# Weights split by accumulating DMAs from GpSimd's queue, and buffers that begin at multiples of 1 KB

## The chip, the cores and the metric

The kernel runs on one core of one Trainium2 chip. The metric is the device time of one execution in microseconds; the time before is the median of three runs. Traces are of one profiled execution on that core.

## What is computed

Two transformer-like blocks in a row on one sequence of 512 tokens of width 1024, all in float32: a block with gated linear attention, three groups of dilated attention, a mixing projection, an MLP and a gated embedding; and a block of two layers, one with mLSTM and stick-breaking attention, one with multi-scale pooling. Cut to the matmuls that carry the time:

```python
def first_block(x, p, ln1, w_in, ...):
    h = rmsnorm(x, ln1[i])
    hq, hk, hv, hr, ha, hatt, hgate = _split_cols(h @ w_in[i], SPLIT_SIZES)
    ...                                   # gla_mixer, dilated_attention x 3
    mix = (jax.nn.sigmoid(g_gla) * y_gla + jax.nn.sigmoid(g_att) * y_att) @ w_out[i]
    x = x + mix
    h2 = rmsnorm(x, ln2[i])
    x = x + jnp.square(jax.nn.relu(h2 @ w_mlp1[i])) @ w_mlp2[i]
    h3 = rmsnorm(x, ln3[i])
    x = x + jax.nn.sigmoid(h3 @ w_pg[i]) * (p[i] @ w_pp[i])
    return rmsnorm(x, ln_f)

def even_layer(...):   # mlstm, stick_breaking
    u = h @ w_in
    ...
    y = jnp.concatenate([ya, yb], axis=-1) @ w_out
    return x + rmsnorm_2(y, post_g)

def odd_layer(...):    # h @ w_in, multiscale_pool, grouped matmul, @ w_out
```

## The kernel before

**Precision.** Every large product is made of three matmuls in fp32r, a rounded form of float32: an operand is split into a high part (rounded to fp32r) and a low part (the rest), and high times high, high times low and low times high are summed in PSUM. `split` (L168) does this for activations: ACT copies with rounding, DVE subtracts. A matmul has 128x128 weights (the stationary operand) and 512 columns of the moving operand.

**Weights.** The host lays all weights out as a stream of chunks of 128x1024 float32 (512 KB), in the order of use; the kernel takes 316 of them. `load_chunk` (L206) loads a chunk by a DMA from SP's queue into a buffer of the ring `raw` (three buffers). `split_chunk` (L213) makes the parts in the rings `wh` and `wl` (four buffers each): ACT copies with rounding (L219), DVE subtracts (L220), and the next load is issued, which waits until that subtract has freed its raw buffer.

**Units.** One unit of work consumes one chunk: 24 matmuls with 512 columns. In `fm` (L330) the weights are stationary and the activations move; in `tok` (L411) the activations are stationary and the weights move. `run` (L284) goes through the program's groups of one to three units; ahead of a group that begins with unit i it calls `split_chunk(i + 3)` (L300), then lets side jobs (attention, gated linear attention, mLSTM, stick-breaking) take their next step by `pump` (L272), then emits the unit's matmuls, and after these the evacuation of its PSUM bank. Side jobs have fixed lags, counted in units (`LAG`). A scheduler then orders each engine's instructions.

**Buffers.** Activations lie in buffers of 2 KB a partition, in three kinds: e (44 buffers), s and r (16 each). In the built program the e buffers and the weight rings begin at 320 bytes past a multiple of 1 KB in each partition, the s and r buffers at 672 bytes past one: the first is a multiple of 64 bytes, the second lies 32 bytes past such a multiple. The products with the MLP's second weights (L780 and L782) read their moving operand from s and r buffers (L757), those with the first weights (L761) from e buffers; the last products (`w_out_c_2`, by `tok`) read their stationary operand from s and r buffers (L1470). Of the 7,534 matmuls with 512 columns in the built program, 1,576 have an operand that begins 32 bytes past a multiple of 64: 1,192 the moving one, 448 the stationary one (64 of them both). With the change there are 26.

**GpSimd (POOL)** has few instructions: the triangular masks of the side jobs (`causal`, L193, a select on 128x128 or 128x256), adds of squares for the norms (`accum`, L499), and a copy in `narrow` (L362). No DMA is issued from its queue. All work of the helper `mm` is at L162, of `act` at L124, of `tt` (the subtracts among it) at L141, of `stt` at L153.

**The start.** `setup` (L508) issues, on SP's queue, the vectors, x's first tile, the first 256 columns of chunks 0 and 1, x's second tile, the other 768 columns, the other six tiles of x, and then chunks from 2 on. `prologue` (L549) splits them in that order, pinned, and chunk 2 after these.

## Time and profile before

| | |
|---|---|
| time, median of 3 runs | 1937.28 us (1932.48 to 1937.69) |
| the profiled execution | 1936.63 us, span of its trace 1934.9 us |
| PE (matmuls) busy | 1911.9 us, 99% of the span |
| PEld (weight loads into the array) busy | 1597.9 us, 83% |
| DVE busy | 1090.2 us, 56% |
| ACT busy | 873.2 us, 45% |
| POOL busy | 94.7 us, 5% |
| DMA | 184.32 MB, mean 95 GB/s |
| granted clock of TensorE | 0.996 of full speed |

Busy time of PE includes the overlap of pipelined matmuls: one of 512 columns is shown with some 390 ns, but a new one begins every 225 to 235 ns in a stretch without idle time, so how many instructions fall into a stretch says more than the busy time. Idle time of an engine is given with what ended it. An engine that is busy 56% of the time may still be the one that PE waits for in a short stretch.

### The profile page before, as it was taken

Reading aid. Unit: us, or ns where it says so; the run is one execution under the profiler, and the core shown is the slowest. Engines: PE = TensorE matmul, PEld = TensorE weight load, DVE = VectorE, ACT = ScalarE, POOL = GpSimd, SP = SyncE. Lnnn points to the kernel's source line nnn. Section 1 sums busy time; section 2 is a strip of 40 time slices with the busy share of each in tenths; the row PEclk is TensorE's granted clock in tenths of the full one; section 3 lists DMA queues with packets and bytes.
Section 4 is the critical chain, followed back from the end, with each engine's and each line's share of the span. In section 5 each row is a group of like instructions: output and inputs, shape, how many; then the busy total and the mean of one; then the engine's idle time right before and its main releaser. Section 6 shows DMA issues by size and latency. Waiting matters only on the chain.

```text
span 1934.9 us, 22678 instructions
## 1 busy us (share of the span) xinstructions
PE 1911.9 (99%) x8894; PEld 1597.9 (83%) x8894; DVE 1090.2 (56%) x1623; ACT 873.2 (45%) x1274; POOL 94.7 (5%) x125
## 2 busy tenths in 40 slices
PE   8999999999999999999998999999999999999998
PEld 7888888888888888888887888888888888888886
DVE  5235544677446433444556768677866627666723
ACT  4233344564234321342355666767666534423321
POOL 0000000000001000000120000111100011000000
PEclk9999999999999999999999999999999999999999
DMA  5342222122242322333232323222222322233222
GB/s 182 126 106 87 83 77 98 66 77 88 92 138 87 109 98 92 107 98 98 88 115 81 120 77 91 73 88 77 88 87 74 126 96 76 87 98 98 96 92 74
DMA packets 68095, 184.32 MB, mean 95 GB/s; under 512 B 17058, under 2 KB 20815, under 8 KB 67988
## 3 DMA queue, kind: packets, MB, share of 16 engines
q1 hardware_dynamic: 67412, 181.82, 29.2%
q8 instruction: 70, 1.15, 0.2%
q10 hardware_dynamic: 576, 1.05, 0.1%
q14 instruction: 37, 0.30, 0.1%
HBM read 178.55 MB, written 6.12 MB: 95 GB/s over the span
## 4 chain that ended last, share of the span: by engine, by line
PE 94%; DVE 3%; ACT 1%; DMA 1%; issue 0%; SPq 0%; POOL 0%; DVEq 0%; ACTq 0%; POOLq 0%
PE t L162 93%; DVE t L141 2%; ACT t L124 1%; DMA t<-t 1%; DVE t L153 1%; PE t L965 0%; DMA t<-wstream 0%; PE t L1528 0%; ACT L124 0%; POOL t L499 0%; PE t L1037 0%; SPq L528 0%; ACT L135 0%; DVE t L1252 0%; SPq L525 0%
## 5 line engine op out<-in xcount | busy, mean ns | idle before, releaser
L162 PE MATMUL t<-t,t 128*128 128x512 f32 (+3 forms) x8532 | 1871.5, 381 | 15.7 <-ACT t L124 9.8
L162 PEld LDWEIGHTS t<-t,t 128*128 128x128 f32 x8532 | 1550.0, 192 | 323.2 <-ACT t L124 13.4
L141 DVE TENSOR_TENSOR t<-t,t 128x1024 fp32r<-128x1024 f32 (+9 forms) x982 | 773.1, 815 | 730.4 <-ACT t L124 404.1
L124 ACT ACTIVATE t<-t 128x1024 fp32r<-128x1024 f32 (+6 forms) x883 | 633.5, 758 | 924.3 <-PE t L162 557.6
L153 DVE SCALAR_TENSOR_TENSOR t<-t,ct,t 128x512 f32<-128x512 f32 (+5 forms) x128 | 102.5, 815 | 14.4 <-ACT t L124 11.2
L153 DVE SCALAR_TENSOR_TENSOR t<-t,t 128x512 f32<-128x512 f32 (+6 forms) x112 | 76.5, 702 | 54.2 <-PE t L162 45.8
L124 ACT ACT_TABLE_LOAD x69 | 88.5, 1283 | 11.2 <-DVE t L153 8.6
L499 POOL TENSOR_TENSOR t<-t,t 128x512 f32<-128x512 f32 x33 | 52.2, 1590 | 581.6 <-ACT t L124 581.3
L124 ACT ACTIVATE t<-t,t 128x128 f32<-128x128 f32 (+4 forms) x93 | 50.3, 545 | 62.8 <-PE t L162 36.7
L124 ACT ACTIVATE t<-t,ct 128x512 f32<-128x512 f32 (+5 forms) x89 | 54.8, 624 | 19.4 <-DVE t L141 12.8
L196 POOL TENSOR_SCALAR_AFFINE_SELECT t<-t 128x128 f32<-128x128 f32 x80 | 37.4, 482 | 418.3 <-ACT t L124 222.5
L141 DVE TENSOR_TENSOR t<-t 128x511 f32<-128x511 f32 (+5 forms) x64 | 37.3, 587 | 1.2
L473 DVE RECIPROCAL t<-t 128x512 f32<-128x512 f32 (+3 forms) x15 | 28.1, 1870 | 13.5 <-ACT t L124 13.5
L153 DVE SCALAR_TENSOR_TENSOR t<-t,t,t 128x512 fp32r<-128x512 f32 (+3 forms) x41 | 27.7, 683 | 13.1 <-ACT t L124 12.8
L162 PE MATMUL t<-t,ct 128*128 128x256 f32 (+4 forms) x142 | 28.6, 337 | 0.0
L162 PEld LDWEIGHTS t<-t,ct 128*128 128x128 f32 (+1 forms) x142 | 21.6, 186 | 3.6 <-issue 1.0
L130 ACT ACTIVATE t<-t 128x512 f32<-128x512 f32 (+2 forms) x25 | 12.4, 561 | 10.3 <-PE t L162 7.7
L162 PEld LDWEIGHTS t<-ct,t 128*128 128x128 f32 x112 | 16.5, 217 | 0.6
L132 ACT ACT_TABLE_LOAD x13 | 16.7, 1283 | 0.2
L162 PE MATMUL t<-ct,t 128*128 128x1 f32 (+1 forms) x112 | 16.2, 276 | 0.0
L1509 ACT ACTIVATE t<-t 128x512 f32<-128x512 f32 x8 | 4.8, 599 | 24.7 <-PE t L162 24.7
L135 ACT ACTIVATE t<-t 128x512 f32<-128x512 f32 (+2 forms) x29 | 15.8, 594 | 0.2
(54 smaller groups left out, 132.9 us busy)
## 6 DMA issues: line engine op xcount, KB each, us to landing
t<-wstream SPq DMA_DIRECT2D x314, 512.0 KB, 3.3
t<-xT SPq DMA_DIRECT2D x16, 256.0 KB, 5.3
xdram<-t SPq DMA_DIRECT2D x8, 256.0 KB
t<-udram SPq DMA_DIRECT2D x8, 256.0 KB
t<-xdram SPq DMA_DIRECT2D x8, 256.0 KB, 6.0
out<-t ACTq DMA_DIRECT2D x4, 256.0 KB, 2.1
out<-t SPq DMA_DIRECT2D x4, 256.0 KB
skew<-bdram SPq DMA_DIRECT2D x2, 510.0 KB
```

Source lines behind the costliest of these rows:

```text
L124: self.pinned(self.nc.scalar.activation(out, in_, func, **kw))
L130: last = self.nc.scalar.activation(o, x, AF.Abs, bias=bias)
L132: last = self.nc.scalar.preload_act_table_set(EXPLN)
L135: last = self.nc.scalar.activation(o, o, AF.Exp, scale=-1.0)
L141: self.pinned(self.nc.vector.tensor_tensor(out, a, b, op=op))
L153: self.pinned(self.nc.vector.scalar_tensor_tensor(out, a, s, b, op0=op0, op1=op1))
L162: self.nc.tensor.matmul(out, lhsT, rhs, start=start, stop=stop, skip_group_check=True)
L196: self.nc.gpsimd.affine_select(t[:, 0:n], t[:, 0:n], pattern=[[1, n]], compare_op=op, fill=0.0, base=base, channel_multiplier=-1)
L473: self.nc.vector.reciprocal(out, out)
L499: self.nc.gpsimd.tensor_tensor(st[key], st[key], sq, op=ALU.add)
L1509: last = nc.scalar.activation(sq, ps, AF.Square, accum_out=ss[j][:, c:c + 1])
```

## The change

- The ring `raw` and the loads on SP's queue are gone (but for chunks 0 and 1). A chunk's high part is loaded by a DMA on POOL's queue that writes fp32r, which rounds on the way.
- The low part: ACT writes the negated high part into the `wl` buffer (in place of the rounding copy), and a second DMA on POOL's queue reads the same chunk from HBM again and adds it to that buffer. DVE's subtract for 314 chunks is gone.
- The rings have five buffers in place of four. The high part of chunk i+4 is loaded, and the low part of chunk i+3 started, ahead of unit i.
- A pad and first uses of the buffer kinds place the buffers of 2 and 4 KB: in the built program all of e, s, r, `wh` and `wl` begin at multiples of 1 KB.
- At the start, chunks 0 and 1 come in three pieces (256, 256 and 512 columns) into s buffers.

```diff
--- before.py
+++ after.py
@@ -54,14 +54,14 @@
 ROUNDS = "a0 z0 a1 a2 z1 a3 z2 z3"
 BANKS = 2
 NCONST = P + 64 + P
-AHEAD = 4
+PAD = 88
 POOLSQ = 1
-PIECES = slice(0, 256), slice(256, 1024)
-HEAD = [("x", 0), ("w", 0), ("x", 1), ("w", 1)] + [("x", k) for k in range(2, KT)]
+PIECES = slice(0, 256), slice(256, 512), slice(512, 1024)
+HEAD = [("x", 0), ("w", 0), ("x", 1), ("w", 1), ("w", 2)] + [("x", k) for k in range(2, KT)]
 
 LAG = {'attention': (2, 5, 2), 'gla': (2, 3, 1, 2, 4), 'ml_gates': (5,), 'mlstm': (4, 0, 2), 'ml_out': (1, 0), 'stick': (0, 3, 3)}
 QBANKS, PER_SLOT = 4, 2
-RAW_BUFS, HL_BUFS = 3, 4
+HL_BUFS, LEAD = 5, 1
 BIASW = (383, 255, 255)
 N_ONEHOT = sum(BIASW)
 
@@ -203,24 +203,23 @@
         return h, l
 
 
+
+
     def load_chunk(self, j):
         while self.nd <= min(j, len(self.units) - 1):
-            t = self.sb.tile([P, 1024], F32, name=self._nm(), tag="raw", bufs=RAW_BUFS)
-            self.nc.sync.dma_start(t, self.io["wstream"][self.nd])
-            self.raw[self.nd] = t
+            h, l = (self.sb.tile([P, 1024], F32R, name=self._nm(), tag=t, bufs=HL_BUFS) for t in ("wh", "wl"))
+            self.nc.gpsimd.dma_start(h, self.io["wstream"][self.nd])
+            self.hl[self.nd] = h, l
             self.nd += 1
 
     def split_chunk(self, j):
         while self.ns <= min(j, len(self.units) - 1):
             self.load_chunk(self.ns)
-            raw = self.raw.pop(self.ns)
-            h = self.sb.tile([P, 1024], F32R, name=self._nm(), tag="wh", bufs=HL_BUFS)
-            l = self.sb.tile([P, 1024], F32R, name=self._nm(), tag="wl", bufs=HL_BUFS)
-            self.act(h, raw, AF.Copy)
-            self.sub(l, raw, h.bitcast(F32))
-            self.hl[self.ns] = (h, l)
+            h, l = self.hl[self.ns]
+            self.act(l, h.bitcast(F32), AF.Copy, scale=-1.0)
+            self.nc.gpsimd.dma_start(l, self.io["wstream"][self.ns], accum_op=ALU.add)
             self.ns += 1
-            self.load_chunk(self.ns - 1 + RAW_BUFS)
+            self.load_chunk(self.ns - 1 + LEAD)
 
 
     def load(self, dst, src):
@@ -297,7 +296,8 @@
                 x()
             else:
                 m = len(x)
-                self.split_chunk(i + HL_BUFS - 1)
+                self.split_chunk(i + HL_BUFS - 2)
+                self.load_chunk(i + HL_BUFS - 1)
                 for _ in range(m):
                     self.pump()
                     if self.jobs:
@@ -504,11 +504,22 @@
         self.act(z, z, AF.Silu)
         return z
 
+    def piece(self, j, k):
+        s = PIECES[k]
+        return self.raw[j][s.start // T][:, s.start % T:s.start % T + s.stop - s.start]
+
 
     def setup(self):
         nc, io = self.nc, self.io
         self.eps = self.C([P, 1])
         nc.vector.memset(self.eps, EPS)
+
+        self.M(1)
+        self.C([P, PAD])
+        for k in "esr":
+            self.S(kind=k)
+        for t in ("wh", "wl"):
+            self.sb.tile([P, 1024], F32R, name=self._nm(), tag=t, bufs=HL_BUFS)
         self.act(self.M(1), self.eps, AF.Square)
         self.vecs = self.C([P, NVEC])
         nc.sync.dma_start(self.vecs, io["vecs"])
@@ -516,7 +527,7 @@
 
 
         for j in range(2):
-            self.raw[j] = self.sb.tile([P, 1024], F32, name=self._nm(), tag="raw", bufs=RAW_BUFS)
+            self.raw[j] = self.S(kind="s"), self.S(kind="s")
             self.hl[j] = tuple(self.sb.tile([P, 1024], F32R, name=self._nm(), tag=t, bufs=HL_BUFS)
                                for t in ("wh", "wl"))
         self.nd = self.ns = 2
@@ -525,8 +536,7 @@
                 nc.sync.dma_start(self.xt[k], io["xT"][k * P:(k + 1) * P, :])
             else:
                 for j in range(2):
-                    nc.sync.dma_start(self.raw[j][:, PIECES[k]], io["wstream"][j][:, PIECES[k]])
-        self.load_chunk(AHEAD)
+                    nc.sync.dma_start(self.piece(j, k), io["wstream"][j][:, PIECES[k]])
         consts = self.C([P, NCONST])
         nc.sync.dma_start(consts, io["consts"])
         self.ident = consts[:, 0:P]
@@ -555,7 +565,7 @@
                 else:
                     for j in range(2):
                         h, l = (t[:, PIECES[k]] for t in self.hl[j])
-                        r = self.raw[j][:, PIECES[k]]
+                        r = self.piece(j, k)
                         self.act(h, r, AF.Copy)
                         self.sub(l, r, h.bitcast(F32))
             self.split_chunk(2)
```

POOL's queue at the start of the program, before (`t` are buffers; `t_156` sums squares, `t_1700` and `t_1701` are a chunk's parts; a name in brackets is the semaphore of the engine, or of the DMA, that is waited for):

```order
L1618 UNCONDITIONAL_BRANCH [waits barrier_Pool_Activation_PE_DVE_SP_gather]
L840 MEMSET ct_398 33x12
L566 ISA
L566 TENSOR_TENSOR t_156<-t_69 128x512 [waits DMAHW1_49]
L362 COPY t_1700<-t_1701 128x8x64 [waits DVE_49]
```

and with the change:

```order
L850 MEMSET ct_403 33x12
L211 DMA t_159<-wstream 128x1024
L211 DMA t_164<-wstream 128x1024
L211 DMA t_192<-wstream 128x1024
L576 ISA
L576 TENSOR_TENSOR t_167<-t_76 128x512 [waits DMAHW1_49]
L220 DMA t_160<-wstream 128x1024 [waits Activation_49]
L220 DMA t_165<-wstream 128x1024 [waits Activation_49]
L220 DMA t_193<-wstream 128x1024 [waits Activation_49]
L211 DMA t_297<-wstream 128x1024 [waits PE_49]
L211 DMA t_302<-wstream 128x1024 [waits DVE_49,PE_49]
L211 DMA t_307<-wstream 128x1024 [waits DMASW0_49,PE_49]
```

L211 is the load of a high part, L220 the accumulating DMA of a low part. Three loads now stand first in the queue, and the low part of the third of the next three chunks stands behind a load that waits for PE.

POOL's queue at the selects of one head of stick-breaking attention, before:

```order
L196 AFFINE_SELECT t_8015<-t_8015 128x128 [waits Activation_49]
L196 AFFINE_SELECT t_8016<-t_8016 128x128 [waits Activation_49]
L196 AFFINE_SELECT t_8017<-t_8017 128x128 [waits Activation_49]
L196 AFFINE_SELECT t_8017<-t_8017 128x256 [waits DVE_49]
L196 AFFINE_SELECT t_7937<-t_7937 128x128 [waits DVE_49]
```

and with the change:

```order
L211 DMA t_7747<-wstream 128x1024 [waits DMASW7_49,PE_49]
L220 DMA t_7708<-wstream 128x1024 [waits DMASW0_49,Activation_49]
L220 DMA t_7748<-wstream 128x1024 [waits DMASW1_49,PE_49,Activation_49]
L211 DMA t_7835<-wstream 128x1024 [waits DMASW2_49,PE_49]
L196 AFFINE_SELECT t_7765<-t_7765 128x128 [waits DVE_49]
L196 AFFINE_SELECT t_7766<-t_7766 128x128 [waits DVE_49]
L196 AFFINE_SELECT t_7767<-t_7767 128x128 [waits DVE_49]
L196 AFFINE_SELECT t_7767<-t_7767 128x256
L220 DMA t_7836<-wstream 128x1024 [waits DMASW3_49,Activation_49]
```

The four selects of a head now stand behind two accumulating DMAs, which wait for ACT, and a load, which waits for PE.

DVE's queue at the end of the first block, where the evacuations of the gated embedding (L811 to L815) run and the normalisation of the next block waits for their last sums, before:

```order
L141 TENSOR_TENSOR t_7234<-t_7099,t_7233 128x1024
L153 SCALAR_TENSOR_TENSOR t_7226<-t_4232,t_7017,t_7225 128x512
L141 TENSOR_TENSOR t_7264<-t_7239,t_7010 128x512
L141 TENSOR_TENSOR t_7280<-t_7145,t_7279 128x1024
L141 TENSOR_TENSOR t_7264<-t_7264,t_7089 128x512
L141 TENSOR_TENSOR t_4234<-t_4234,t_7264 128x512
L153 SCALAR_TENSOR_TENSOR t_7272<-t_4234,t_7017,t_7271 128x512
L141 TENSOR_TENSOR t_7310<-t_7285,t_7010 128x512
L141 TENSOR_TENSOR t_7326<-t_7191,t_7325 128x1024
```

and with the change:

```order
L153 SCALAR_TENSOR_TENSOR t_7069<-t_4154,t_6865,t_7068 128x512
L141 TENSOR_TENSOR t_7106<-t_7081,t_6858 128x512
L141 TENSOR_TENSOR t_7106<-t_7106,t_6935 128x512
L141 TENSOR_TENSOR t_4156<-t_4156,t_7106 128x512
L153 SCALAR_TENSOR_TENSOR t_7114<-t_4156,t_6865,t_7113 128x512
L141 TENSOR_TENSOR t_7151<-t_7126,t_6858 128x512
L141 TENSOR_TENSOR t_7151<-t_7151,t_6937 128x512
```

The subtracts of 128x1024 elements, one per chunk, no longer stand between the steps of the evacuations.

## Rows read from the trace of the kernel before

**Rows 1.** The page: span, busy time by engine, shares of the chain.
```profile
span 1934.9 us, 22678 instructions
...
PE 1911.9 (99%) x8894; PEld 1597.9 (83%) x8894; DVE 1090.2 (56%) x1623; ACT 873.2 (45%) x1274; POOL 94.7 (5%) x125
...
PE 94%; DVE 3%; ACT 1%; DMA 1%; issue 0%; SPq 0%; POOL 0%; DVEq 0%; ACTq 0%; POOLq 0%
```

**Rows 2.** Windows: busy us (xcount) of PE, PEld, DVE, ACT, POOL; clock; DMA; GB/s.
```profile
700.00:775.00 75.00, 75.00 (x323) 60.37 (x322) 24.39 (x26) 13.79 (x13) 0.00 (x0) 1.00 0.30 99
1700.00:1775.00 75.00, 75.00 (x333) 62.11 (x332) 44.80 (x76) 23.65 (x30) 0.00 (x0) 1.00 0.31 99
1850.00:1925.00 75.00, 75.00 (x321) 60.31 (x320) 19.48 (x26) 17.66 (x26) 0.00 (x0) 1.00 0.19 63
```

**Rows 3.** The page: largest DMA queue; weight loads (KB, us to landing).
```profile
q1 hardware_dynamic: 67412, 181.82, 29.2%
...
t<-wstream SPq DMA_DIRECT2D x314, 512.0 KB, 3.3
```

**Rows 4.** By form, DVE: count, busy us, mean ns, idle before and why.
```profile
L141 DVE TENSOR_TENSOR t<-t,t 128x1024 fp32r<-128x1024 f32 x314 | 385.3, 1228 | 334.9 <-ACT t L124 326.0 <-PE t L162 6.9 <-POOL t L499 0.8
```

**Rows 5.** By form, ACT: the same columns.
```profile
L124 ACT ACTIVATE t<-t 128x1024 fp32r<-128x1024 f32 x314 | 331.6, 1059 | 738.0 <-PE t L162 538.1 <-issue 178.3 <-DMA t<-wstream 13.6
```

**Rows 6.** Windows over the stretches in which PE waits.
```profile
0.00:31.00 31.00, 25.31 (x103) 19.90 (x104) 19.70 (x30) 19.43 (x28) 1.34 (x6) 1.00 0.71 243
997.00:1029.00 32.00, 28.50 (x161) 24.60 (x160) 28.13 (x33) 18.95 (x31) 14.82 (x10) 0.98 0.36 124
1029.00:1067.00 38.00, 36.53 (x189) 31.82 (x189) 23.42 (x41) 23.36 (x29) 0.00 (x0) 0.93 0.19 66
...
1598.00:1636.00 38.00, 34.84 (x251) 33.02 (x249) 29.65 (x57) 20.15 (x38) 8.17 (x6) 0.91 0.17 53
```

**Rows 7.** DVE by form in 997 to 1029 us.
```profile
L141 DVE TENSOR_TENSOR t<-t,t 128x512 f32<-128x512 f32 x16 | 14.4, 911 | 3.9 <-ACT t L124 3.7
L141 DVE TENSOR_TENSOR t<-t,t 128x1024 fp32r<-128x1024 f32 x6 | 9.3, 1555 | 1.3 <-POOL t L499 0.8 <-ACT t L124 0.5
```

**Rows 8.** DVE by form in 1602.5 to 1628 us.
```profile
L141 DVE TENSOR_TENSOR t<-t,t 128x256 f32<-128x256 f32 x32 | 15.0, 518 | 1.4 <-PE t L162 1.4
L153 DVE SCALAR_TENSOR_TENSOR t<-t,ct,t 128x256 fp32r<-128x256 f32 x16 | 9.6, 612 | 0.2 <-ACT t L124 0.2
L141 DVE TENSOR_TENSOR t<-t,t 128x1024 fp32r<-128x1024 f32 x2 | 2.4, 1208 | 0.0
```

**Rows 9.** Timeline, first microseconds: start, duration, work, [idle before].
```profile
9.30 0.84 ACT L124 ACTIVATE t<-t 128x768 fp32r<-128x768 f32 x1 [0.18 <-DMA t<-wstream]
...
11.85 13.71 PE L162 MATMUL t<-t,t 128*128 128x512 f32 x59 [0.55 <-DVE t L153]
14.64 7.55 ACT L124 ACTIVATE t<-t 128x1024 fp32r<-128x1024 f32 x11 [0.57 <-DMA t<-wstream]
```

**Rows 10.** Windows over the first loads, columns as in rows 2.
```profile
3.00:6.00 3.00, 0.86 (x2) 0.57 (x2) 1.15 (x2) 1.03 (x2) 1.04 (x1) 1.00 0.84 238
...
12.00:15.00 3.00, 3.00 (x14) 2.43 (x15) 3.00 (x5) 2.43 (x5) 0.00 (x0) 1.00 1.05 411
```

**Rows 11.** POOL's selects: count, ns (min, median, max), from when to when.
```profile
L196 POOL TENSOR_SCALAR_AFFINE_SELECT t<-t x80: 292/297/1388, 1078.1 to 1476.7; 128x128 f32<-128x128 f32 x60, 128x256 f32<-128x256 f32 x20
...
  ACT t L124: 4.7, 4
```

**Rows 12.** Timeline, one chain with selects, up to the PE.
```profile
1101.73 1.63 POOL L196 TENSOR_SCALAR_AFFINE_SELECT t<-t 128x128 f32<-128x128 f32 x2 [0.31 <-DVE t L153]
1101.79 3.79 DVE L141 TENSOR_TENSOR t<-t,t 128x1024 fp32r<-128x1024 f32 x5
...
1105.84 1.54 DVE L141 TENSOR_TENSOR t<-t,t 128x1024 fp32r<-128x1024 f32 x2
...
1109.99 2.30 PE L162 MATMUL t<-t,ct 128*128 128x512 f32 x14
```

## The prediction

> **What bounds the kernel now.** I read the page first: the span is 1934.9 us, PE is busy 99% of it, and 94% of the chain of work that ended last lies on PE [rows 1]. So the time is set by how many matmuls there are, how far apart they begin, and the few stretches in which PE waits. The profiled execution took 1936.63 us, 1.7 us more than its span and 0.65 us less than the median of 1937.28; the sum below is made against the span, with 1.7 us put back at its end.
>
> Next I counted matmuls in windows of 75 us in which PE never idles. From 1700 us there are 333, so one begins every 75/333 = 225 ns. From 700 us (the MLP's second weights) there are 323, or 232 ns, and from 1850 us (`w_out_c_2`) 321, or 234 ns [rows 2]. All run at a granted clock of 1.00. The slow windows are those in which one operand lies in s or r buffers, which begin 32 bytes past a multiple of 64. So there are two rates, 7.0 to 8.4 ns apart.
>
> Last come the stretches in which PE waits: the start (25.3 us busy of 31), 997 to 1029 (28.5 of 32, clock 0.98), 1029 to 1067 (36.5 of 38, clock 0.93) and 1598 to 1636 (34.8 of 38, clock 0.91) [rows 6]. In all others the subtracts of the weights are hidden: 314 of them take 385.3 us of DVE [rows 4], of a span in which DVE is 56% busy [rows 1].
>
> **Alignment.** The change moves all buffers to multiples of 1 KB: of 1,576 matmuls with an operand at an odd multiple of 32 bytes 26 are left, so 1,550 go to the fast rate, if the start address is what sets the rate. At 7.0 ns (the difference in rows 2 for the window at 700 us, which has the form of the 1,192 with such a moving operand) this gives 1,550 x 7.0 ns = 10.9 us, taken as **-11**. At 8.4 ns it would be -13.0; if what makes them slow is something else about those buffers, 0. PE is the bound there and nothing waits, so the whole of it counts.
>
> **DVE's subtracts.** Removed are 314 x 1.228 us [rows 4], nearly all hidden behind PE. They count in two places only. From 997 to 1029 us DVE is busy 28.1 of 32 us [rows 6], in the evacuations of the gated embedding and the norm that PE waits for; 6 subtracts take 9.3 us there [rows 7], in front of the steps of that chain. PE idles 3.5 us there and 1.5 in the next 38, and the granted clock of 0.98 and 0.93 loses up to 0.02 x 32 + 0.07 x 38 = 3.3 more [rows 6]: a clock that comes back with PE's waits gone would return it. The bounds are 0 and -8.3; **-4**, since adds of 128x512 (16, 14.4 us) remain in the chain [rows 7]. Next late there is ACT, busy 19.0 of the 32 us [rows 6]. From 1602.5 to 1628 us 32 adds of 128x256 and 16 multiplications with an add fill 24.6 of 25.5 us of DVE, and 2 subtracts 2.4 us [rows 8] (the parts exceed the window by what begins inside it and ends behind). PE idles 3.2 us around it, and a clock of 0.91 costs 0.09 x 38 = 3.4 [rows 6]. Bounds 0 and -6.6; **-2.4**, the subtracts alone.
>
> **ACT** has as many passes as before: a negation of 128x1024 from SBUF to SBUF in place of a rounding copy of that size, 1.059 us [rows 5]. Nothing is counted for it; ACT is 45% busy [rows 1] and hides it.
>
> **The start.** Three loads of 512 KB now stand first in POOL's queue, beside SP's loads of x and of chunks 0 and 1. From 3 us on the DMA engines are nearly full, 238 GB/s rising to 411 GB/s at 12 to 15 us [rows 10]; 1.57 MB at 400 GB/s are 3.9 us. Before, those bytes came behind x. If all of them went ahead of SP's, the last split of the first chunks (768 columns at 9.30 us, PE's stream from 11.85 [rows 9]) would move by 3.9 us. Two more pieces cost ACT little: 0.84 us for 768 columns [rows 9] against perhaps 0.3 + 0.6 for two parts, and the smaller last piece could gain up to 0.3. Chunk 2's split, before at 14.64 us [rows 9], now ends with a second load, 3.3 us from issue to landing [rows 3], some 2 us more than DVE's 1.23. Bounds -0.3 and +6; **+3**, the middle. The Trainium skill, "DMA: Bandwidth & Descriptors", § Issuing engines are not separate DMA queues, says that DMAs of all issuers run on the same 16 engines and interleave; by it neither queue goes first, and half of 3.9, some 2 us, would be the delay. No row of before has two large queues at once.
>
> **The chain of a chunk.** New is: load (3.3 us [rows 3]), negation (1.06 [rows 5]), accumulating DMA. Its time stands in no row. It reads the chunk again and must read and write the buffer; between the time of a load, 3.3, and twice that, 6.6, the chain has 7.7 to 11.0 us. A unit of 24 matmuls has 24 x 225 ns = 5.4 us [rows 2]. A buffer released by unit i-1 is needed by unit i+4, so 21.6 us are there, and the chain is hidden. Only after the two groups of three units are the next two chunks served within two units, 10.8 us; there one chunk could be 11.0 + 3.3 (behind another's load) - 10.8 = 3.5 us late, twice: 0 to +7, **+2** taken, nearer to none.
>
> **Transfers.** Of q1's 181.82 MB a chunk's 0.524 cost 29.2% x 1934.9 x 0.524/181.82 = 1.63 us of all 16 engines [rows 1, 3]. Load and accumulation at that price are 3.3 us per unit of 5.4, so the DMA engines are not the bound; nothing is counted, and the other case is a rival.
>
> **The sum**: 1934.9 - 11 - 4 - 2.4 + 3 + 2 = 1922.5 us of span, with the 1.7 us outside it 1924 us, 0.7% below the median.
>
> **Rivals.** (1) The address is not the cause, or the new waits eat what it brings: without the -11 the sum is 1935.2, within 0.3% of the median (0.3%, 5.8 us, is about what a measurement of this kernel can tell from no change). For it: the slow windows also differ in program place, and the s and r buffers in their region of SBUF. Against: moving and stationary operands, in different stages, show about the same loss [rows 2]. From 1932 to 1943.
>
> (2) **Slower: POOL's queue holds the selects.** 628 DMAs now stand in POOL's queue in order, and each waits for PE to release a buffer, for ACT's negation, or for the eighth DMA back. Behind them stand 80 selects of stick-breaking attention, 1078 to 1477 us [rows 11], in 20 groups of four. A group that must wait until PE finishes a unit is a unit, 5.4 us, late. At 1101.8 us DVE did two subtracts of some 1.2 us in that chain ([rows 12], duration by rows 4), which the change gives back, 2.45 us; what is left is 3 us for each group that is held, and it decides from a hold of 2.45 us on. All 20 held: +60, some 1984; half, +30, 1954. For it: the order puts two accumulations and a load directly before the selects. Against: side jobs lag by units, ACT waited for selects only 4.7 us in all [rows 11], and the loads wait for a unit that is already done in most cases. The Trainium skill, same page, § SWDGE vs HWDGE vs iDMA, says that the GpSimd writes a DMA's descriptors in software, into SBUF that VectorE can lock it out of; by it each DMA would hold POOL's queue longer, by a time that no row here shows.
>
> (3) **Slower: the accumulating DMA is the bound.** If it costs three times a plain load on the engines, a unit needs 1.63 + 4.89 = 6.52 us against 5.4, and it decides from (5.4 - 1.63)/1.63 = 2.3 times on. Then 314 x 6.52 = 2,047 us, with the start some 2,060 to 2,100. For it: nothing of that kind was in the trace. Against: its bytes are those of a load and one more read and write of SBUF. The Trainium skill, same page, § Rules for kernel authors, says that such a DMA reads its destination and writes it later. Two transfers by that are 2 x 1.63 = 3.3 us, a unit 4.9 < 5.4, and the forecast stands.
>
> (4) **Much faster.** If buffers at multiples of 1 KB let matmuls follow each other closer than any do now, by a second step as large as that between 234 and 225 ns, 7,534 x 9 ns = 68 us more go: 1924 - 68 = 1856. The Trainium skill, "TensorE: Matmul & The Clock Gate", § Wait — 56ns, not 53.3ns?, gives 215.7 ns for 512 columns once warm; by it 7,534 x (225 - 215.7) ns = 70 us would go. Against: the fast rate, 225 ns, already belongs to buffers that begin at multiples of 64 bytes [rows 2].
>
> **How the numbers follow.** Forecast (1912 to 1932, the sum with one or two terms at a bound): 0.60. Rival 1: 0.15. Rival 2: 0.12. Rival 3: 0.10. Rival 4: 0.03. The time is the forecast's, 1924. The range leaves out rivals 3 and 4, the upper third of rival 2 and the forecast's edges: 1912 to 1965, some 8 in 10. Below 1931.5: the forecast but for its upper edge, and rival 4: 0.62. Above 1943.1: rivals 2 and 3, 0.22. Between: 0.16.
>
> **What would show it.** Right: a 75 us window of 512-column matmuls without idle time has some 333 of them, at 700 and 1850 us too; no large subtract on DVE; windows like 997 to 1029 shorter; an accumulating DMA of 3.3 to 6.6 us from issue to landing; PE's idle time without DMA as the releaser. Wrong: 323 in those windows (rival 1), PE waits from 1078 to 1477 that end with POOL or with ACT behind a select (rival 2), the DMA share near 1 and PE waiting for the accumulations throughout (rival 3), or 345 in those that have 333 now (rival 4).

## The result: slower by 18%

The changed kernel takes 2278.06 us (median of 4 runs, 2275.85 to 2284.6) against 1936.88 us before (median of 4 runs): a ratio of 1.177, 95% interval 1.174 to 1.180. The prediction was 1924 us, faster, with a range up to 1965. The time lies 341 us above the kernel before and 313 us above the range.

From the page of the changed kernel: the span; busy time by engine; POOL's DMA queue (packets, MB, share of 16 engines); the shares of the chain that ended last; the weight DMAs (both kinds, KB, median us from issue to landing).

```profile
span 2278.3 us, 22843 instructions
...
PE 1997.9 (88%) x8894; PEld 1646.9 (72%) x8894; DVE 729.9 (32%) x1311; ACT 865.9 (38%) x1274; POOL 526.6 (23%) x753
...
q0 software_dynamic: 90432, 329.29, 63.3%
...
issue 49%; PE 17%; DMA 13%; POOL 12%; ACT 5%; DVE 3%; POOLq 0%; SPq 0%; ACTq 0%; DVEq 0%
...
t<-wstream POOLq DMA_DIRECT2D x628, 512.0 KB, 6.1
```

PE was busy 1911.9 of 1934.9 us before [rows 1], so it idled 23 us. Now it idles 2278.3 - 1997.9 = 280 us. It is also busy 86 us longer with the same 8,894 matmuls, at a mean granted clock of 0.941 in place of 0.996. The chain lies on PE for 17%, where it was 94% [rows 1]; half of it is "issue", time for which the profile shows no cause of the wait. The DMA engines are not full: POOL's queue takes 63.3% of them. Every chunk but the first two is now moved twice: 329.29 MB in this queue.

The waits of the changed kernel: who waits for whom, us in all, times, the longest.

```profile
POOL t L220 <- ACT t L124: 1364.7, 288, 13.5
ACT t L124 <- DMA t<-wstream: 1058.3, 220, 11.2
...
POOL t L211 <- PE t L162: 233.3, 68, 34.0
```

POOL's accumulating DMAs (L220) wait 1365 us for ACT, which has not yet negated; ACT waits 1058 us for loads. Before, ACT waited for loads only 13.6 us ahead of its weight copies [rows 5]. One piece of POOL's timeline shows what repeats (start, duration, line, operation, count, idle time before and what ended it; L211 is a load).

```profile
2063.37 0.85 POOL L220 DMA_DIRECT2D t<-wstream  x1 [8.01 <-ACT t L124]
2063.92 1.42 POOL L211 DMA_DIRECT2D t<-wstream  x2
2071.97 0.88 POOL L220 DMA_DIRECT2D t<-wstream  x1 [6.63 <-ACT t L124]
2073.44 0.87 POOL L220 DMA_DIRECT2D t<-wstream  x1 [0.60 <-ACT t L124]
2073.99 0.89 POOL L211 DMA_DIRECT2D t<-wstream  x1
2082.65 0.85 POOL L220 DMA_DIRECT2D t<-wstream  x1 [7.78 <-ACT t L124]
```

From 2063.37 to 2082.65, in 19.3 us, three loads and three accumulations are issued, 6.4 us for a chunk, where PE needs 5.4 [rows 2]. POOL stands still twice, 6.63 and 7.78 us, each time at an accumulation whose negation waits for a load that was issued just ahead. Behind it in the queue stand the next loads; in this piece none of them has idle time of its own before it. The times from issue to landing (min, median, max), first of the loads, then of the accumulations:

```profile
DMA to landing us min/median/max: 3.4/6.5/11.0
```

```profile
DMA to landing us min/median/max: 5.1/5.5/14.6
```

A load has 6.5 us at the median, against 3.3 before [rows 3]. Two windows, at the start and in the MLP (columns as in rows 2):

```profile
0.00:31.00 31.00, 22.82 (x85) 17.40 (x85) 14.04 (x26) 16.05 (x26) 7.40 (x15) 1.00 0.78 223
900.00:1000.00 100.00, 90.21 (x380) 72.54 (x378) 13.78 (x20) 21.31 (x25) 22.49 (x33) 0.97 0.72 169
```

At 900 us PE gets 380 matmuls done in 100 us, 6.3 us for a unit of 24, with a granted clock of 0.97. POOL issues 15 accumulations in these 100 us, 6.2 us from one to the next: the queue sets the pace.

To see where the 341 us come from, the start of the matmul with the same number was compared between the traces. The number is the place among all 8,894 matmuls of a trace in order of time; the rows are at numbers up to which all these traces have run the same kinds of matmul equally often, since in between their order differs. The table has the start in the kernel before and how much later it is in the others (negative: earlier); the runs are explained below.

| matmul no. | before, us | buffers moved only | changed kernel | two chunks ahead | both, attention in order | changed, attention in order |
|---|---|---|---|---|---|---|
| 300 | 76 | 1.9 | 12.0 | 6.9 | 7.6 | 12.3 |
| 600 | 145 | 0.9 | 16.8 | 5.6 | 6.3 | 16.8 |
| 1300 | 280 | 0.9 | 103.1 | 64.5 | 25.2 | 56.1 |
| 4400 | 972 | -6.3 | 203.9 | 57.5 | 18.3 | 160.7 |
| 4710 | 1035 | -7.3 | 211.3 | 53.9 | 13.2 | 168.0 |
| 7440 | 1608 | -7.6 | 304.4 | 54.3 | 13.3 | 258.4 |
| 7750 | 1667 | -6.2 | 300.9 | 53.0 | 12.6 | 254.9 |
| last | 1929 | -9.1 | 343.3 | 50.2 | 9.7 | 302.7 |

The changed kernel loses nearly everywhere, some 15 us per 100 in the long stretches (1300 to 4400, 4710 to 7440, and from 7750 on), and 86 us in one place, the 135 us from matmul 600 to 1300, where the four heads of dilated attention run.

### The profile page after: what moved, and what is told of

Read it like the earlier page. It is cut to its first block, busy times and chain, and to the rows that moved or that the text cites. A ratio compares the mean times of both kernels' runs of the same rounds, so it can differ in the third digit from the quotient of the medians.

```text
span 2278.3 us, 22843 instructions
## 1 busy us (share of the span) xinstructions
PE 1997.9 (88%) x8894; PEld 1646.9 (72%) x8894; DVE 729.9 (32%) x1311; ACT 865.9 (38%) x1274; POOL 526.6 (23%) x753
## 3 DMA queue, kind: packets, MB, share of 16 engines
q0 software_dynamic: 90432, 329.29, 63.3%
## 4 chain that ended last, share of the span: by engine, by line
issue 49%; PE 17%; DMA 13%; POOL 12%; ACT 5%; DVE 3%; POOLq 0%; SPq 0%; ACTq 0%; DVEq 0%
PE t L162 17%; DMA t<-wstream 12%; POOL t L220 5%; POOL t L211 5%; ACT t L124 4%; DVE t L141 2%; DVE t L153 1%; POOL t L499 1%; ACT L124 1%; DMA t<-xT 1%; POOL t L196 1%; ACT t L135 0%; ACT L132 0%; DMA udram<-t 0%; DMA t<-udram 0%
## 5 line engine op out<-in xcount | busy, mean ns | idle before, releaser
L162 PE MATMUL t<-t,t 128*128 128x512 f32 (+3 forms) x8532 | 1949.7, 390 | 184.6 <-DMA t<-wstream 79.4
L162 PEld LDWEIGHTS t<-t,t 128*128 128x128 f32 x8532 | 1594.1, 198 | 524.0 <-DMA t<-wstream 94.7
L124 ACT ACTIVATE t<-t 128x1024 fp32r<-128x1024 f32 (+8 forms) x885 | 630.5, 755 | 1312.5 <-DMA t<-wstream 1058.3
L141 DVE TENSOR_TENSOR t<-t,t 128x512 f32<-128x512 f32 (+8 forms) x670 | 397.2, 618 | 933.9 <-ACT t L124 455.8
L220 POOL DMA_DIRECT2D t<-wstream x314 | 273.1, 873 | 1400.7 <-ACT t L124 1364.7
L211 POOL DMA_DIRECT2D t<-wstream x314 | 232.9, 792 | 235.6 <-PE t L162 233.3
L153 DVE SCALAR_TENSOR_TENSOR t<-t,ct,t 128x512 f32<-128x512 f32 (+5 forms) x128 | 107.9, 857 | 108.7 <-ACT t L124 105.6
L975 PE MATMUL t<-ct,t 128*128 128x128 f32 x60 | 14.2, 397 | 59.5 <-DVE t L157 59.5
L124 ACT ACTIVATE t<-t,ct 128x512 f32<-128x512 f32 (+6 forms) x89 | 54.8, 624 | 25.7 <-DVE t L141 14.4
L975 PEld LDWEIGHTS t<-ct,t 128*128 128x128 f32 x60 | 11.6, 209 | 62.2 <-DVE t L157 61.4
L196 POOL TENSOR_SCALAR_AFFINE_SELECT t<-t 128x128 f32<-128x128 f32 x80 | 32.5, 429 | 54.9 <-DVE t L153 30.0
L162 PEld LDWEIGHTS t<-ct,t 128*128 128x128 f32 x112 | 16.7, 222 | 12.0 <-ACT t L124 6.2
```

The lines of the kernel that those rows point to most:

```text
L124: self.pinned(self.nc.scalar.activation(out, in_, func, **kw))
L141: self.pinned(self.nc.vector.tensor_tensor(out, a, b, op=op))
L153: self.pinned(self.nc.vector.scalar_tensor_tensor(out, a, s, b, op0=op0, op1=op1))
L162: self.nc.tensor.matmul(out, lhsT, rhs, start=start, stop=stop, skip_group_check=True)
L196: self.nc.gpsimd.affine_select(t[:, 0:n], t[:, 0:n], pattern=[[1, n]], compare_op=op, fill=0.0, base=base, channel_multiplier=-1)
L211: self.nc.gpsimd.dma_start(h, self.io["wstream"][self.nd])
```

## Experiment: the buffers alone

The kernel before, with the pad and the first uses of the change and nothing else.

```diff
+PAD = 88
...
+        self.M(1)
+        self.C([P, PAD])
+        for k in "esr":
+            self.S(kind=k)
+        for t in ("wh", "wl"):
+            self.sb.tile([P, 1024], F32R, name=self._nm(), tag=t, bufs=HL_BUFS)
+        self.sb.tile([P, 1024], F32, name=self._nm(), tag="raw", bufs=RAW_BUFS)
```

> The kernel before with the buffers moved to multiples of 1 KB (the pad and the first uses of the change), nothing else; 26 matmuls of 512 columns keep an operand at an odd multiple of 32 bytes. If the start address sets the rate (1,550 matmuls x 7.0 to 8.4 ns): 1924 to 1926 us, and some 333 matmuls in the windows of 75 us that now have 321 to 323. If something else makes them slow: 1937 and the same counts.

Measured: 1927.08 us, ratio 0.9946 (0.9933 to 0.9958), 10 us less. Windows of this run, the MLP's second weights and the last products:

```profile
700.00:775.00 75.00, 75.00 (x333) 62.14 (x332) 26.22 (x28) 14.86 (x14) 0.00 (x0) 1.00 0.30 97
1840.00:1915.00 75.00, 75.00 (x332) 62.13 (x332) 19.17 (x24) 17.30 (x25) 0.00 (x0) 1.00 0.20 64
```

There are 333 and 332 matmuls in 75 us where before there were 323 and 321 [rows 2]. The step of the sum holds, at -10 for the -11 predicted. No other kernel of this study has a lower time.

## Experiments: what stops POOL's queue

**Two chunks ahead.** The high part of chunk i+5 is loaded when the low part of chunk i+3 is started; the rings have six high and four low buffers in place of five each.

```diff
-HL_BUFS, LEAD = 5, 1
+H_BUFS, L_BUFS, LEAD = 6, 4, 2
...
-                self.split_chunk(i + HL_BUFS - 2)
-                self.load_chunk(i + HL_BUFS - 1)
+                self.split_chunk(i + L_BUFS - 1)
```

> The changed kernel with two chunks' high parts loaded ahead of the chunk whose low part is started, in place of one; six high and four low buffers in place of five each, so the same memory. Theory Q (POOL's queue in its order: an accumulation waits for a negation, that for a load which was issued just before, so each round trip of 8 to 9 us stops the queue): the round trip is spread over two chunks and most of the 341 us go: 1930 to 2050. Rival D (the 16 DMA engines: an accumulation costs more of them than a load, and the bytes bound the time): at least 2200.

Measured: 1991.36 us, ratio 1.0287 (1.0271 to 1.0302): 287 of the 341 us are gone, with the same DMAs. From its page (as above) and its waits:

```profile
span 1985.2 us, 22895 instructions
...
PE 1908.1 (96%) x8894; PEld 1600.2 (81%) x8894; DVE 730.1 (37%) x1311; ACT 871.6 (44%) x1276; POOL 523.6 (26%) x753
...
q0 software_dynamic: 90432, 329.29, 76.6%
```

```profile
POOL t L211 <- PE t L162: 1029.3, 272, 32.7
...
POOL t L222 <- ACT t L124: 306.6, 289, 14.5
```

The accumulations wait for ACT 307 us in all in place of 1365, and POOL now stands at loads that wait for PE to release a buffer, 1029 us: PE sets the pace. The DMA engines are busier than in the changed kernel, 76.6%, so their bytes were not the bound. In its window from 900 to 1000 us they are 91% busy, though, and little room is left. The table shows the shape: from matmul 1300 on this kernel loses nothing more.

**The second DMA without adding.** It writes the buffer in place of adding to it (the low part is then the whole weight).

```diff
-            self.nc.gpsimd.dma_start(l, self.io["wstream"][self.ns], accum_op=ALU.add)
+            self.nc.gpsimd.dma_start(l, self.io["wstream"][self.ns])
```

> The changed kernel with the second DMA of a chunk writing its buffer in place of adding to it; the low part is then the whole weight, so it is only for the time. All waits stay, the negation too. Theory Q: the queue's stops stay, only shorter DMAs: 2150 to 2260. Rival D: if the accumulation's price is the bound, two plain loads at 1.63 us of the 16 engines need 3.3 us of a unit's 5.4, and PE is the bound again: 1925 to 1960.

Measured: 2011.94 us, ratio 1.0395 (1.0379 to 1.0411), below what theory Q gave and above what rival D gave: 266 us are gone though all waits stayed. The page, and the loads from issue to landing:

```profile
span 2009.8 us, 22843 instructions
...
q0 software_dynamic: 90432, 329.29, 53.1%
```

```profile
DMA to landing us min/median/max: 3.4/4.6/11.7
```

The share gives an estimate of the DMAs' price: 53.1% of 2009.8 us for 628 plain ones are 1.70 us each of the 16 engines. In the changed kernel 63.3% of 2278.3 us are 1442 us; less 314 x 1.70 that leaves 2.89 us for an accumulation, 1.7 times a load; the 76.6% of 1985.2 us with two chunks ahead leave 3.14, 1.85 times. A unit needs 4.6 to 4.8 us of the DMA engines, under PE's 5.4, so rival 3, which decides from 2.3 times a load on, is not what bounds. But a load that is issued right behind an accumulation lands in 6.5 us at the median, with a plain DMA there in 4.6. That the two share the engines is the likely reason; no run takes it apart. The stops of the queue are about as long as that landing. So the cause is the order of the queue and the price of the accumulation together: either one taken away brings the loop near or under PE's 5.4 us, which the expectation for theory Q did not see.

**No negation.** POOL sets the low buffer to zero by a memset, and the DMA adds the whole weight; POOL's queue no longer waits for ACT, nor ACT for a load.

```diff
-            self.act(l, h.bitcast(F32), AF.Copy, scale=-1.0)
+            self.nc.gpsimd.memset(l.bitcast(F32), 0.0)
```

> The changed kernel with a memset to zero on POOL in place of ACT's negation, so that the accumulation adds the whole weight; all DMAs and their bytes stay, but POOL's queue no longer waits for ACT, nor ACT for a load. Theory Q: PE is the bound again: 1925 to 1970. Rival D: nothing falls, 2200 to 2280.

Measured: 1991.85 us, ratio 1.0283 (1.0269 to 1.0297). Its page:

```profile
span 1991.9 us, 22575 instructions
...
PE 1907.1 (96%) x8894; PEld 1600.3 (80%) x8894; DVE 729.3 (37%) x1311; ACT 564.5 (28%) x961; POOL 819.5 (41%) x1067
...
q0 software_dynamic: 90432, 329.29, 76.1%
```

With one chunk ahead, the accumulation in place and its full traffic, PE is busy 96%. So the loop runs through the negation: load, ACT, accumulation, next load. With that link cut it is gone; what remains is the place at the attention, which this run shares with the two before it.

## Experiments: the order at the attention

What two chunks ahead leave is lost between matmuls 600 and 1300. The program's order shows why, and it is so in the changed kernel too: before, the transposes of the four heads stand on PE after 576, 720, 864 and 1000 matmuls of 512 columns; with the change after 880, 929, 976 and 1020. The scheduler moved them, and left some 45 matmuls, two units, between heads. PE's timeline with two chunks ahead, then that of before, at the first transposes of a head (L976, then L965):

```profile
248.50 3.25 PE L976 MATMUL t<-ct,t 128*128 128x128 f32 x15 [22.41 <-DVE t L157]
...
282.00 2.23 PE L976 MATMUL t<-ct,t 128*128 128x128 f32 x9 [11.31 <-DVE t L157]
...
309.95 0.48 PE L976 MATMUL t<-ct,t 128*128 128x128 f32 x1 [7.08 <-DVE t L157]
```

```profile
233.54 1.80 PE L965 MATMUL t<-ct,t 128*128 128x128 f32 x15
...
272.79 1.80 PE L965 MATMUL t<-ct,t 128*128 128x128 f32 x15
```

Now PE idles 22, 11 and 7 us ahead of these three heads, and 10 at the fourth (340.2 us), each time until DVE has done a step of the head's chain through DVE, ACT and small DMAs; before, it idled at none of the four. The first run keeps PE's matmuls of that stretch in program order.

```diff
+    def ordered(self, ins):
+        return self.tc.keep_in_program_order(ins) if self.in_order else ins
...
-        self.nc.tensor.matmul(out, lhsT, rhs, start=start, stop=stop, skip_group_check=True)
+        self.ordered(self.nc.tensor.matmul(out, lhsT, rhs, start=start, stop=stop, skip_group_check=True))
...
+        self.do(lambda: self.set_order(True))
         self.go(self.attention(0, AT, VT))
```

> The kernel with two chunks loaded ahead, and PE's matmuls kept in program order while the four heads of attention run: a head's transposes then stand after 576, 720, 864 and 1000 matmuls of 512 columns, as in the kernel before, in place of after 880, 929, 976 and 1020. Theory O (the order that the scheduler chose leaves the heads two units apart, less than a head's chain through ACT, DVE and small DMAs takes, so PE waits): the 57 us lost between 217 and 282 us of before's time go, 1930 to 1940. Rival: the small DMAs of attention are slowed by POOL's big ones wherever they stand; then at least half of it stays: 1960 to 1990.

Measured: 1968.75 us, ratio 1.016 (1.0146 to 1.0174): 23 us less, not 57. The transposes stood in their old places, but not what they wait for. DVE, and then PE, at the first head:

```profile
160.10 1.08 DVE L149 TENSOR_TENSOR t<-t,t 128x512 f32<-128x512 f32 x1 [4.35 <-PE t L170]
161.09 0.29 DVE L905 CUSTOM_DVE_ANT_0 t<-t,t 128x128 f32<-128x128 f32 x1
```

```profile
181.17 3.51 PE L986 MATMUL t<-ct,t 128*128 128x128 f32 x15 [21.10 <-DVE t L165]
```

DVE's score reductions (L905) stand behind an evacuation that waits for the unit which ends at 160.1, just ahead of the transposes, and PE waits 21 us. With PE alone in order and one chunk ahead (the same edit on the changed kernel) nothing was gained:

> The changed kernel (one chunk ahead) with PE's matmuls kept in program order in the same place. Theory Q and O together: some 57 us go, the stops of POOL's queue stay: 2190 to 2235. If the waits at the attention are only another face of the queue's stops, nothing changes: 2265 to 2285.

Measured: 2286.82 us, against 2278 without (ratios 1.1806, 1.1782 to 1.1829, and 1.1773, 1.1741 to 1.1804); the 57 us of the first expectation did not go. The next run keeps ACT and DVE in order as well.

```diff
-        self.in_order = on
+        self.in_order = self.pin = on
...
-            nc.vector.tensor_tensor_reduce(dst[:, lo:lo + n], ps[:, lo:lo + n], bias, scale=1.0, scalar=-3e38,
+            self.pinned(nc.vector.tensor_tensor_reduce(dst[:, lo:lo + n], ps[:, lo:lo + n], bias, scale=1.0,
...
```

> As the run with two chunks ahead and PE in order during attention, with ACT's and DVE's instructions of that stretch in program order too. In the run with PE alone in order, DVE's score reductions of the first head still stood behind the evacuation of the last unit ahead of that head's transposes (161 us), so PE waited 21 us there. Theory O: with the whole chain in its place the loss of 22 us at the first head and of 18 us behind it goes: 1930 to 1942. Rival (the small DMAs of attention are slow beside POOL's big ones, wherever they stand): 1955 to 1970.

Measured: 1948.43 us, ratio 1.0062 (1.0049 to 1.0076), 43 us less than with two chunks ahead alone and 6 us above the expectation. The page, and PE's timeline at the first two heads:

```profile
span 1944.7 us, 22882 instructions
...
PE 1906.5 (98%) x8894; PEld 1596.8 (82%) x8894; DVE 730.2 (38%) x1311; ACT 868.5 (45%) x1276; POOL 524.4 (27%) x753
```

```profile
157.28 1.22 PE L170 MATMUL t<-t,t 128*128 128x512 f32 x2 [4.81 <-DVE t L149]
161.44 7.64 PE L170 MATMUL t<-t,t 128*128 128x512 f32 x22 [2.94 <-DMA t<-wstream]
168.93 1.80 PE L987 MATMUL t<-ct,t 128*128 128x128 f32 x15
170.48 35.03 PE L170 MATMUL t<-t,t 128*128 128x512 f32 x176
...
210.94 1.80 PE L987 MATMUL t<-ct,t 128*128 128x128 f32 x15
```

PE passes the transposes (L987) without idle time. Ahead of the first head it still idles 4.8 us for DVE and 2.9 us for a weight DMA. These and the last head make the 19 us that are left of this place (6.3 to 25.2 in the table). The program's order is not the scheduler's order of before: there the first head's reductions began at 86.8 us, here at 128.1, behind an evacuation at 127.4 that waited for PE. What else the order of before has that this one lacks was not tried. The rival, slow small DMAs, is not borne out for the 2 KB DMAs of attention, which landed in 8.4 us (median, 60 to 300 us) before and in 6.4 here:

```profile
t<-skew SPq DMA_DIRECT2D x4, 128.0 KB, 32.8
...
t<-t SPq DMA_DIRECT2D x32, 2.0 KB, 6.4
```

It is partly so for the score bias that the reductions read (`t<-skew`): its first DMA landed here 32.8 us after its issue, at 123.6 us, and before it was there by 86.8. Here the reductions waited 4.5 us longer for the evacuation, so the bias was not their last wait; with a better order it would be the next.

The same order with one chunk ahead tells whether the two losses add:

> The changed kernel (one chunk ahead) with PE, ACT and DVE in program order during attention. If the losses of the queue and of the order add: some 43 us less than the changed kernel's 2278, so 2225 to 2245. If the queue's stops hold the attention up whatever its order: 2270 to 2300, as with PE alone in order.

Measured: 2241.49 us, ratio 1.1581 (1.1558 to 1.1604), 37 us less than the changed kernel. In its dense stretch (columns as in rows 2) the queue's pace is that of the changed kernel:

```profile
900.00:1000.00 100.00, 89.83 (x377) 72.40 (x376) 18.49 (x27) 29.88 (x41) 22.43 (x32) 0.97 0.70 165
```

The two losses add, within some 6 us: from 2278 by the order -37, by two chunks ahead -293 more, 1948; the other way round -287 and -43.

## Experiments: the start

Two runs put POOL's first three loads behind its square of x's first tile, which waits for that tile.

```diff
+            sqs = [self.S() for k in range(POOLSQ)]
+            for k in range(POOLSQ):
+                self.pinned(nc.gpsimd.tensor_tensor(sqs[k], self.xt[k], self.xt[k], op=ALU.mult))
+            self.load_chunk(4)
             self.split_chunk(2)
```

> As the run with two chunks ahead and attention in order, with POOL's first three loads behind its square of x's first tile, which waits for that tile. If these loads delay the start (the first 300 matmuls come 6.9 us late with two chunks ahead, 1.9 us with the buffers' move alone): 3 to 5 us less than without. If x and chunks 0 and 1 are late for another reason: no difference.

> The same with POOL's first three loads behind its square of x's first tile: PE's first matmul comes at 5 us as before in place of 7. By the run that had this alone, 1.5 to 3 us less than without it; if theory O holds, 1926 to 1938, on a level with the kernel before in which only the buffers were moved (1927).

Measured: 1967.08 us (ratio 1.0153, 1.0139 to 1.0167) against 1968.75, and 1945.22 us (1.0044, 1.0032 to 1.0057) against 1948.43. PE's first matmul comes at 5.1 and 5.2 us in place of 7.2 and 6.7, so these loads do delay it; of the whole time it is 2 to 3 us, where 3 to 5 and 1.5 to 3 were expected, and the intervals overlap, so the gain is not settled. The second run lies 7 us above its expected 1926 to 1938, as the one without it lies above its own. No kernel with the DMA split came under the kernel before.

## Experiments: what the two rates hang on

The prediction put the slower rate down to operands that begin 32 bytes past a multiple of 64. Two runs shift everything in the aligned kernel (PAD = 96 and 104 in place of 88), by 32 and by 64 bytes.

> The kernel before with its buffers moved as in the change and then by 32 bytes more: all 7,534 matmuls of 512 columns read operands that begin 32 bytes past a multiple of 64 (and of 1 KB). If the address sets the rate: 7,340 x 6.6 ns = 48 us more than the aligned kernel's 1927, so 1970 to 1980. If the s and r buffers are slow because of where they lie and not of the 32 bytes: 1927 to 1937.

> The kernel before with its buffers moved by 64 bytes past the multiples of 1 KB. If a multiple of 64 bytes is enough: 1925 to 1929, as with multiples of 1 KB. If multiples of 1 KB are wanted: up to 1975.

Measured: 1927.77 us (0.9955, 0.9941 to 0.9968) and 1928.71 us (0.9957, 0.9942 to 0.9972), both as fast as the aligned one. With all operands at +32 bytes:

```profile
700.00:775.00 75.00, 75.00 (x333) 62.10 (x332) 26.22 (x28) 14.86 (x14) 0.00 (x0) 1.00 0.30 96
1840.00:1915.00 75.00, 75.00 (x333) 62.10 (x332) 19.40 (x24) 16.84 (x24) 0.00 (x0) 1.00 0.20 64
```

So an odd multiple of 32 bytes costs nothing by itself. Three runs move s and r alone against the rest, by 64, 32 and 352 bytes, with a constant of that size behind the first use of e and another, up to 1 KB, ahead of the weights.

```diff
+        self.S(kind="e")
+        self.C([P, 16])
+        for k in "sr":
+            self.S(kind=k)
+        self.C([P, 240])
```

> The kernel before with e buffers and weights at multiples of 1 KB, s and r buffers 64 bytes past them. If the two operands' starts must differ by a multiple of 64 bytes: 1926 to 1929 and 333 matmuls in a window of 75 us of the MLP's second weights. If they must begin at the same offset in 1 KB: 1935 to 1939 and 323.

> The same with s and r buffers 32 bytes past the multiples of 1 KB. If a difference of an odd multiple of 32 bytes between the operands' starts is what costs: 1935 to 1939 and 323 matmuls in such a window. If the place of the buffers in the kernel before was the cause: 1926 to 1929 and 333.

> The same with s and r buffers 352 bytes past the multiples of 1 KB, which is their distance from the others in the kernel before. If the difference between the starts is the cause, in whichever unit: 1935 to 1939, the time of before, and 323 matmuls in such a window. If not: 1926 to 1929.

Measured: 1930.08 us (0.9967, 0.9955 to 0.9978), 1936.30 us (0.9999, 0.9989 to 1.0008) and 1936.65 us (1.0002, 0.9992 to 1.0012). The two windows, for s and r at +64 and at +32:

```profile
700.00:775.00 75.00, 75.00 (x329) 61.56 (x328) 25.91 (x28) 14.86 (x14) 0.00 (x0) 1.00 0.29 95
1840.00:1915.00 75.00, 75.00 (x323) 60.40 (x323) 17.45 (x21) 16.68 (x23) 0.00 (x0) 1.00 0.20 64
```

```profile
700.00:775.00 75.00, 75.00 (x324) 60.21 (x323) 23.77 (x27) 14.10 (x14) 0.00 (x0) 1.00 0.30 97
1840.00:1915.00 75.00, 75.00 (x323) 60.36 (x322) 18.57 (x22) 16.76 (x21) 0.00 (x0) 1.00 0.21 70
```

At +32 and at +352 (323 and 322 in these windows) the whole gain is gone. At +64 it is partly there: 329 matmuls where the moving operand is shifted, but 323 where the stationary one is. So at the distances tried it is the distance between the two operands' starts that sets the rate, and neither rule of the expectation for +64 is right alone: at a distance of 64 bytes a shifted moving operand costs 75/329 - 75/333 = some 3 ns, at 32 bytes 6, a shifted stationary one 7 at both.

## Why the prediction was wrong, step by step

**Alignment (-11).** Right in size (-10) and in place. Wrong in the mechanism: not where an operand begins decides, but that both begin at the same offset (0, 32, 64 and 320 bytes past a multiple of 512 are alike). That the number came out was luck in this: the change puts both operands at the same offset as well as at multiples of 64. The trace of before could not tell these apart, since only one pair of offsets was in it.

**DVE's subtracts (-4 and -2.4).** In size as predicted, seen in the runs that are not held by the queue. From matmul 4400 to 4710 the kernel with two chunks ahead and attention in order gains 5.1 us, the one with the buffers moved 1.0: 4.1 by the subtracts. From 7440 to 7750 it is -0.7 against +1.4: 2.1. With two chunks ahead alone they are 2.6 and 2.7. These are differences of traces; no run took the subtracts alone. The windows that answer to 997 to 1029 and 1029 to 1067 us [rows 6] in that kernel:

```profile
1015.00:1043.00 28.00, 26.18 (x150) 22.94 (x149) 18.08 (x24) 16.97 (x26) 18.81 (x20) 1.00 1.01 228
1043.00:1080.00 37.00, 35.35 (x202) 30.44 (x201) 20.32 (x38) 25.75 (x35) 7.29 (x11) 1.00 0.82 183
```

DVE is busy 18 of 28 us where it was 28 of 32, and the clock is at 1.00 where it was 0.98 and 0.93.

**ACT (nothing).** Failed. The duration is as before (1.057 us, x314), but the pass was costed as work, not as a wait: what ACT copied before had been loaded three chunks ahead; what it negates is loaded just before, and ACT waits 1058 us for it, with all that stands behind it in its queue.

**The start (+3).** Within its bounds: the first 300 matmuls are 7 us late with two chunks ahead, 1.9 with the buffers alone. Some 5 us are the split's. In the changed kernel itself they are 12.0 late, since the queue's stops begin here.

**The chain of a chunk (+2).** This is the step that failed, by 285 us. It added up one chunk's latency, 7.7 to 11.0 us, and compared it with the 21.6 us between a buffer's release and its use: a chunk would come in time. But the order of POOL's queue, which the text of the change shows (each accumulation stands behind its load, and the next load behind that), lets a chunk's load start only when the accumulation ahead of it has been issued. Then the latency is no longer hidden by what is in flight; it is a period. Loads land in 6.5 us at the median and more in the piece shown; from a load's issue to that of its accumulation it is 8 to 9 us at each stop, and two stops make the 19.3 us for three chunks. Rival 2 named this queue, and asked only what it does to the selects: ACT waits for these 4.8 us in all, 4.7 before [rows 11].

**Transfers (nothing).** Half right. The Trainium skill, "DMA: Bandwidth & Descriptors", § Rules for kernel authors, says that an accumulating DMA reads its destination and writes it later; taken as two transfers, the estimate in the prediction was 3.3 us of the 16 engines. The shares give 2.9 to 3.1, so the trace about agrees, and the engines are not full. But the price counts in the length of each stop, as the run without adding shows.

**What the sum left out.** PE's order was taken as unchanged. It was not, at four places, and with two chunks ahead keeping the order gave back 43 us. The order of the built program could be read beforehand; the places shown there were those of DVE and POOL only.

**The sum, made again:** from the aligned kernel's 1927.1, +21 for the start and the rest of attention less the subtracts (1948.4), +43 for the order at the attention (1991.4), +287 for the queue's stops (2278.1). Rival 4 did not come: where both operands begin alike, a matmul of 512 columns follows in 75/333 = 225 ns, as before. The Trainium skill, "TensorE: Matmul & The Clock Gate", § Wait — 56ns, not 53.3ns?, has 215.7 ns; no run here shows that.

## What to carry to other kernels

When work moves to an engine's queue that runs in order, cost the period of that queue, not the latency of one item: write down what each entry waits for, and ask how many items are in flight at each stop. One more load ahead of its use was worth 287 us here, at the same memory and the same bytes. And when a scheduler sets the order, compare the order of the bounding engine before and after first; a change far from it can move it.

## What the runs showed of the hardware

- A matmul of 128x512 in fp32r begins every 225 to 226 ns where moving and stationary operand begin at the same offset modulo 512 bytes (offsets 0, 32, 64 and 320), and 3 to 8 ns later in the rows where they don't (32, 64 or 352 bytes apart): 321 to 329 in 75 us against 332 and 333. Other distances were not tried.
- An accumulating DMA from HBM into SBUF of 512 KB takes 2.9 to 3.1 us of the 16 engines, a plain one on the same queue 1.7 (estimates from the queue's share). On the page its issue holds POOL for 0.87 us at the median, that of a plain one for 0.53 in the run without adding.
- PE's waits are paid twice: 257 us more of idle time, and 86 us more of busy time at a mean granted clock of 0.941 for the same matmuls. Behind a wait of 2.8 us, which ended at 2065.2, the granted clock is 0.50 (1.2 GHz) up to 2067.9, and matmuls begin every 0.43 us. In all, 243 of those with 512 columns are followed 0.40 to 0.46 us later by the next, 17 before; at 0.2 us each that is an estimate of some 45 of the 86 us.
